# Second half's output projection between the steps of the first half's h, and a later x scaling and earlier rope angles, in a two-block fp32 transformer

## The chip, the cores and the metric

One core of one Trainium2 chip. The metric is the device time of one execution in microseconds (us), the median of several runs.

## What is computed

Two transformer blocks on one sequence of 1024 tokens of width 1024, everything in fp32. The first block has two layers, the second one layer of mixers and a feed-forward part. Cut to what matters here:

```python
# first block: layer 0 is differential attention, layer 1 latent attention; 8 heads each
for i in range(2):
    shift, scale, gate = modulation(c, ada_w[i], ada_b[i])
    h = rmsnorm(x, norm_g[i]) * (1 + scale) + shift
    y = attention_i(h, positions, ...)        # ends in: (o * silu(z)) @ w_out[i]
    x = x + gate * y
x = rmsnorm(x, final_norm_g)
# second block
cos, sin = rope_tables(positions_2)           # cos, sin of positions_2 * inv_freq
h = rmsnorm_2(x, g_mix) * (1 + scale1) + shift1
y = mixers(h @ w_in, cos, sin, ...) @ w_out   # gating, stick-breaking, dilated windows
x = x + (1 + gate1) * y
h = rmsnorm_2(x, g_ffn) * (1 + scale2) + shift2
x = x + (1 + gate2) * feed_forward(h)
return rmsnorm_2(x, g_final)
```

## The kernel before

x is held transposed (features on the 128 partitions, eight tiles of 128 features) and in two halves of 512 tokens. An fp32 product is made of three matmuls on rounded upper parts and their remainders (`mm3`, L192: upper by upper, upper by lower, lower by upper), so one output tile of 128 features by 512 tokens, with eight blocks of the sum, is 24 matmuls 128x512. A weight block comes by a DMA from SyncE (L182), its upper part by a cast on ScalarE (L183), its lower part by a subtraction on GpSimd (L169, through `lo`).

A layer's end is written like this. `out_proj` is a generator with eight steps for a half: weights, 24 matmuls, `scalar_tensor_tensor` on VectorE that adds the gated result to x (the eviction, L781), squares on ScalarE and their sum (`stat_acc`: L372 for the first, L375 and the add L376 for the others), and after some steps a store of x (L788). When a half is done, `stat_sum` casts the sum of squares to an upper part on ScalarE (L383), and two matmuls with ones sum it over the partitions (L386, L387); logarithm and exponential give the root (L393, L394). `make_h` then makes the next layer's input in eight steps: a product on VectorE (L424), for even steps an activation and a subtraction on VectorE (L433, L434), for odd ones two operations on ScalarE and the subtraction on GpSimd (L429, L430, L169). In layer 1 the sum has two forms (with and without the second gain) and three more small operations (L1194, L1195, L1197), and behind make_h eight `scalar_tensor_tensor` scale x for the second block's residual (L1200), followed by stores of it (`move_xt`, L412) and, for the first half, by the rope tables of `positions_2`. The rope tables (L250 to L279) are angles reduced on VectorE (nine operations on 128x1024), then an absolute value, a table load, two sines and a table load on ScalarE.

The code of a layer's end is written half by half: all of the first half's projection, its statistic and h, then all of the second half's. The order in which the engines run is not that: a scheduler puts instructions of the program on each engine by the order of the code and by when it thinks that inputs and buffers are ready, within a priority window, and packs the tiles into SBUF by their lifetimes. Each engine then works strictly in its order, SyncE's queue of DMAs too. Behind the first block, `mixers` begins with two steps of `mixer_a` (its gate, L1215 to L1218, and a normalisation with L1247, L1255 to L1261) before the first queries and keys.

## Time and profile before

| what | us |
|---|---|
| median of three runs | 2959.03 |
| lowest and highest run | 2955.31, 2968.55 |
| the profiled execution itself | 2964.13 |
| span in its trace | 2962.4 |
| TensorE busy in the span | 2646.8 |
| mean granted TensorE clock (1 is full) | 0.951 |

TensorE is busy for 89% of the span. VectorE has 71%, ScalarE 49%, GpSimd 44%. A share is an average over stages with different limits, so the rows further down are taken from single stages: from the ends of the two layers, and from the start.

### The profile page before, as it was taken

The page shows a single profiled execution, that of the slowest core. Times are in us where ns is not written, and L with a number is a line of the kernel's source. Part 1 is how long each engine was busy: PE and PEld are TensorE (multiplying, and loading weights), DVE is VectorE, ACT ScalarE, POOL GpSimd, SP SyncE. Part 2 cuts the span into 40 slices and gives each one's busy share as a digit, 9 for nine tenths or more (in the row PEclk, how much of TensorE's full clock was granted, in tenths as well). Part 3 has the DMA queues.
Part 4 walks back from the last instruction along what each step waited for, and adds up shares of the span by engine and source line. Part 5 has one row for each costly group of instructions (what it writes and reads, how often), then busy time and mean ns, then how long its engine had stood idle before and what let it go on. Part 6 is the DMA issues. An engine that isn't in the chain of part 4 may idle for free. (4 is left out here: it accounts for less than half of the span.)

```text
span 2962.4 us, 34674 instructions
## 1 busy us (share of the span) xinstructions
PE 2646.8 (89%) x12023; PEld 2136.0 (72%) x12023; DVE 2118.1 (71%) x2888; ACT 1437.1 (49%) x2609; POOL 1291.4 (44%) x775
## 2 busy tenths in 40 slices
PE   7889999899889989999987798887887999997897
PEld 4677777777777767787876587776776777775776
DVE  7687677766653377777677665578868888889874
ACT  5455455555543445454554454467544444444432
POOL 3233333333253352122234332244547887778760
PEclk8899999999999999999998899999998999998998
DMA  7534323233351263333333237424441222234564
GB/s 270 142 90 114 92 66 110 75 79 100 106 172 58 66 226 120 114 104 103 109 126 94 74 93 104 101 64 126 130 152 42 80 79 78 82 105 161 189 237 143
DMA packets 316850, 338.91 MB, mean 114 GB/s; under 512 B 37684, under 2 KB 240516, under 8 KB 316676
## 3 DMA queue, kind: packets, MB, share of 16 engines
q1 hardware_dynamic: 316676, 336.70, 38.6%
q8 instruction: 96, 1.57, 0.2%
q14 instruction: 78, 0.64, 0.1%
HBM read 231.17 MB, written 60.89 MB: 99 GB/s over the span
## 5 line engine op out<-in xcount | busy, mean ns | idle before, releaser
L192 PE MATMUL m<-h,wh 128*128 128x512 f32 x4744 | 1398.8, 404 | 62.3 <-ACT wh L183 16.2
L192 PEld LDWEIGHTS m<-h,wh 128*128 128x128 f32 x4744 | 910.4, 194 | 270.9 <-ACT wh L183 18.8
L192 PE MATMUL m<-h,wl 128*128 128x512 f32 x1472 | 589.8, 402 | 8.8 <-POOL wl L169 8.8
L169 POOL TENSOR_TENSOR wl<-wr,wh 128x1024 fp32r<-128x1024 f32 (+1 forms) x146 | 330.5, 2270 | 479.0 <-ACT wh L183 183.7
L761 ACT CAST pt<-m 128x256 fp32r<-128x256 f32 (+1 forms) x632 | 222.3, 370 | 289.9 <-PE m L757 158.3
L192 PEld LDWEIGHTS m<-h,wl 128*128 128x128 f32 x1472 | 286.9, 195 | 73.9 <-POOL wl L169 11.2
L169 DVE TENSOR_TENSOR pt<-m,pt 128x256 fp32r<-128x256 f32 (+2 forms) x652 | 256.3, 416 | 83.1 <-ACT pt L761 70.8
L741 ACT ACTIVATE e<-s,cf 128x1024 f32<-128x1024 f32 x192 | 214.9, 1121 | 155.1 <-DVE cf L738 139.1
L737 DVE TENSOR_REDUCE cf<-s 128x1 f32<-128x1024 f32 x192 | 232.4, 1217 | 75.8 <-PE s L682 40.5
L757 PE MATMUL m<-cr,e 128*128 128x128 f32 x1240 | 195.4, 282 | 32.9 <-DVE cf L738 14.3
L865 POOL TENSOR_SCALAR e<-e,cf 128x1024 f32<-128x1024 f32 x64 | 82.0, 1281 | 307.8 <-DVE cf L742 278.1
L192 PE MATMUL s<-h,wh 128*128 128x512 f32 x720 | 183.3, 400 | 36.4 <-DVE h L169 17.1
L681 PE MATMUL s<-kk,qq 128*128 128x512 f32 (+3 forms) x376 | 152.5, 411 | 52.6 <-ACT e L741 24.9
L757 PEld LDWEIGHTS m<-cr,e 128*128 128x128 f32 x1240 | 152.6, 145 | 61.5 <-issue 22.3
L1533 DVE SCALAR_TENSOR_TENSOR e<-z,cf,e 128x1023 f32<-128x1023 f32 (+1 forms) x88 | 175.8, 2008 | 24.8 <-ACT e L1531 24.6
L192 PE MATMUL m<-pt,v 128*128 128x512 f32 x768 | 188.7, 395 | 1.0 <-DVE pt L169 0.5
L192 PEld LDWEIGHTS s<-h,wh 128*128 128x128 f32 x720 | 136.9, 192 | 72.7 <-DVE h L169 18.6
L183 ACT CAST wh<-wr 128x1024 fp32r<-128x1024 f32 (+2 forms) x134 | 122.1, 915 | 110.6 <-PE m L192 47.2
L192 PEld LDWEIGHTS m<-pt,v 128*128 128x128 f32 x768 | 144.4, 190 | 32.3 <-DVE pt L169 1.6
L1105 POOL TENSOR_SCALAR e<-e,cf 128x1024 f32<-128x1024 f32 x64 | 73.7, 1154 | 186.6 <-DVE cf L742 182.7
L682 PE MATMUL s<-kk,qq 128*128 128x512 f32 (+3 forms) x376 | 144.4, 392 | 1.5 <-DMA qq<-pt 1.5
L169 DVE TENSOR_TENSOR wh<-wl,wh 128x512 fp32r<-128x512 f32 x90 | 121.7, 1370 | 19.4 <-ACT wh L443 19.2
(368 smaller groups left out, 4549.2 us busy)
## 6 DMA issues: line engine op xcount, KB each, us to landing
wr<-in_w_out_dram SPq DMA_DIRECT2D x48, 512.0 KB
tb<-in_w_ada_dram SPq DMA_DIRECT2D x48, 512.0 KB
wr<-in_w_up_dram SPq DMA_DIRECT2D x47, 512.0 KB
wr<-in_w_in_dram SPq DMA_DIRECT2D x45, 512.0 KB
qq<-ab SPq DMA_DIRECT2D x144, 128.0 KB
wr<-in_ada_w_dram SPq DMA_DIRECT2D x32, 512.0 KB
tf<-act SPq DMA_DIRECT2D x30, 512.0 KB
wr<-in_w_down_dram SPq DMA_DIRECT2D x30, 512.0 KB
```

Of the source, the lines that this page charges most:

```text
L169: (eng or self.nc.vector).tensor_sub(lo, src, hi.bitcast(F32))
L183: nc.scalar.copy(hi, raw)
L192: self.nc.tensor.matmul(out, l, r, start=start and n == 0, stop=stop and n == last)
L681: nc.tensor.matmul(ps, q(0, j), kk[:, ks], start=True, stop=False)
L682: nc.tensor.matmul(ps, q(1, j), kk[:, ks], start=False, stop=stop)
L737: nc.vector.reduce_max(nm, ps, axis=AX, negate=True)
L741: nc.scalar.activation(e, ps, AF.Exp, bias=nm, scale=scale, accum_out=sm)
L757: nc.tensor.transpose(ps[:, i], p[:, kt * 128:(kt + 1) * 128], self.ident)
L761: nc.scalar.copy(hi, ps[:, i:i + m])
L865: nc.gpsimd.tensor_scalar(e1, e1, r1, self.neglam, ALU.mult, ALU.mult)
L1105: nc.gpsimd.tensor_scalar(e, e, r, 1.0, ALU.mult, ALU.mult)
L1533: nc.vector.scalar_tensor_tensor(t[:, sh:], u[:, 0:S - sh], col(i), t[:, sh:], ALU.mult, ALU.add)
```

## The change

Four edits. First, `make_h` becomes a generator (`steps_h`); at both layers' ends two of the eight steps of the second half's projection are emitted before the first half's statistic, and the other six alternate with the eight steps of the first half's h. Second, in layer 1 the scaling of x and its stores go to a generator `keep_x` that is emitted in the mixers, alternating with the first queries, keys and values. Third, the rope tables are split into angles and sines; those of `positions_2` are emitted before layer 1's last head's projection (behind `drain(mods)`), with the angles on GpSimd: a cast, multiplications, a subtraction, three pairs of a multiplication into a tile of its own and an addition, and a clamp, eleven operations. Two operations on the way are fused into one, in the first table too. Fourth, two steps of the first queries go between the first two steps of `mixer_a`.

```diff
     def rope_tables(self, nme):
+        self.rope_sin(self.rope_angles(nme, self.nc.vector))
+
+    def rope_angles(self, nme, eng):
...
-        nc.vector.tensor_scalar_mul(k, ang, 1.0 / two_pi)
-        nc.vector.tensor_scalar_add(k, k, magic)
-        nc.vector.tensor_scalar_sub(k, k, magic)
+        eng.tensor_scalar(k, ang, 1.0 / two_pi, magic, ALU.mult, ALU.add)
+        eng.tensor_scalar_sub(k, k, magic)
         for cc in (c1, c2, c3):
-            nc.vector.scalar_tensor_tensor(ang, k, -cc, ang, ALU.mult, ALU.add)
-        nc.vector.tensor_scalar(ang, ang, lim, -lim, ALU.min, ALU.max)
+            if eng is nc.vector:
+                eng.scalar_tensor_tensor(ang, k, -cc, ang, ALU.mult, ALU.add)
+            else:
+                t = self.t("e", [128, S])
+                eng.tensor_scalar_mul(t, k, -cc)
+                eng.tensor_add(ang, ang, t)
+        eng.tensor_scalar(ang, ang, lim, -lim, ALU.min, ALU.max)
+        return ang, k
+
+    def rope_sin(self, angles):
...
     def make_h(self, xt, rr, acol, bcol, scaled=None):
-        nc = self.nc
         out = []
+        drain(self.steps_h(out, xt, rr, acol, bcol, scaled))
+        return out
+
+    def steps_h(self, out, xt, rr, acol, bcol, scaled=None):
...
             out.append((h[:, 0], h[:, 1]))
-        return out
+            yield
...
-        res = []
+        res = [[], []]
         for half in range(2):
             drain(proj[half])
-            res.append(self.make_h(xbox[half][1], self.stat_end(acc[:, half], D), acol, self.mod["shift1"]))
+            if half == 0:
+                drain(some(proj[1], 2))
+            steps = self.steps_h(res[half], xbox[half][1], self.stat_end(acc[:, half], D), acol, self.mod["shift1"])
+            drain(steps if half else alternate(steps, some(proj[1], 6)))
         return res
...
         drain(mods)
+        self.phase = 2
+        self.rope_sin(self.rope_angles("positions_2", nc.gpsimd))
+        self.phase = 1
...
-        hts = []
+        hts = [[], []]
+        self.later = []
         for half in range(2):
             drain(proj[half])
+            if half == 0:
+                drain(some(proj[1], 2))
...
-            hts.append(self.make_h(xt, rf, acol_f, m2["shift_m"]))
-            for c in range(8):
-                nc.vector.scalar_tensor_tensor(xt[c], xt[c], fg[:, c:c + 1], rr, ALU.mult, ALU.mult)
-            self.move_xt(self.xs2, half, tiles, True)
-            if half == 0:
-                self.rope_tables("positions_2")
+            steps = self.steps_h(hts[half], xt, rf, acol_f, m2["shift_m"])
+            drain(steps if half else alternate(steps, some(proj[1], 6)))
+            self.later.append((half, tiles, xt, rr))
         return hts
+
+    def keep_x(self, half, tiles, xt, rr):
+
+        fg = self.col["final_norm_g"]
+        for c in range(8):
+            self.nc.vector.scalar_tensor_tensor(xt[c], xt[c], fg[:, c:c + 1], rr, ALU.mult, ALU.mult)
+            yield
+        self.move_xt(self.xs2, half, tiles, True)
...
         box, vbox = [], []
+        first = qkv(0, box, vbox)
         next(ma)
+        drain(some(first, 2))
         next(ma)
-        drain(alternate(qkv(0, box, vbox), some(ma, 4)))
+        drain(alternate(alternate(first, some(ma, 4)), chain(*(self.keep_x(*x) for x in self.later))))
```

What the scheduler makes of it is seen best at three places. In the rows a line is that of the program they are from; the changed program's lines are 13 to 33 higher from `make_h` on (L424 is L441 there, L434 is L451, L781 is L798, L788 is L805, L376 is L389, L741 is L758; the scaling L1200 is L1233).

SyncE at layer 0's end, before: loads for the next layer (`in_w_in1`), the store of the second half's first tile of x (L788), the last three blocks of the projection's weights (`in_w_out0`).

```order
L182 DMA wr_1223_7696<-in_w_in1_dram 128x8x128
L182 DMA wr_1232_7762<-in_w_in1_dram 128x8x128
L788 DMA xs1_6129<-pt_1135_7087 128x2x512
L182 DMA wr_1165_7272<-in_w_out0_dram 128x8x128
L182 DMA wr_1170_7308<-in_w_out0_dram 128x8x128
L182 DMA wr_1175_7343<-in_w_out0_dram 128x8x128
L788 DMA xs1_6129<-pt_1136_7088 128x2x512
```

The same place now:

```order
L805 DMA xs1_6128<-ab_1047_6560 128x2x512
L182 DMA wr_1153_7211<-in_w_out0_dram 128x8x128
L805 DMA xs1_6128<-pt_1121_7038 128x2x512
L182 DMA wr_1159_7251<-in_w_out0_dram 128x8x128
L182 DMA wr_1166_7292<-in_w_out0_dram 128x8x128
L182 DMA wr_1172_7332<-in_w_out0_dram 128x8x128
L182 DMA wr_1194_7431<-in_w_in1_dram 128x8x128
L182 DMA wr_1197_7438<-in_w_in1_dram 128x8x128
```

The store (L805) is still ahead of the last three weight blocks, but it is that of the two products that are emitted first, and the next layer's loads come behind all of the projection's weights.

VectorE at layer 1's end behind the first half's statistic, before (kk is the first half's x, pt the second's, z the statistic, tf and h4 the products and parts of h):

```order
L1197 TENSOR_TENSOR z_1969_12087<-z_1969_12087 128x512
L424 SCALAR_TENSOR_TENSOR tf_2111_12870<-kk_2031_12379,cf_226,z_1969_12087 128x512 x2
L424 SCALAR_TENSOR_TENSOR tf_2114_12880<-kk_2032_12380,cf_226,z_1969_12087 128x512 x2
L424 SCALAR_TENSOR_TENSOR tf_2117_12890<-kk_2033_12381,cf_226,z_1969_12087 128x512 x2
L424 SCALAR_TENSOR_TENSOR tf_2120_12900<-kk_2034_12382,cf_226,z_1969_12087 128x512 x2
L781 SCALAR_TENSOR_TENSOR pt_2127_12940<-m_2138_12988,cf_226,pt_2127_12940 128x512
L1200 SCALAR_TENSOR_TENSOR kk_2031_12379<-kk_2031_12379,cf_226,z_1969_12087 128x512 x2
L1200 SCALAR_TENSOR_TENSOR kk_2032_12380<-kk_2032_12380,cf_226,z_1969_12087 128x512 x2
L434 SCALAR_TENSOR_TENSOR h4_2112_12872<-tf_2111_12870,cf_226,h4_2112_12872 128x512
L1200 SCALAR_TENSOR_TENSOR kk_2033_12381<-kk_2033_12381,cf_226,z_1969_12087 128x512 x2
L1200 SCALAR_TENSOR_TENSOR kk_2034_12382<-kk_2034_12382,cf_226,z_1969_12087 128x512 x2
L781 SCALAR_TENSOR_TENSOR pt_2128_12941<-m_2144_13026,cf_226,pt_2128_12941 128x512
```

The same place now:

```order
L1223 TENSOR_TENSOR z_1976_12109<-z_1976_12109 128x512
L441 SCALAR_TENSOR_TENSOR tf_2132_12972<-kk_2038_12401,cf_226,z_1976_12109 128x512 x2
L389 TENSOR_TENSOR z_1977_12110<-z_1977_12110,tf_2138_13009 128x512
L798 SCALAR_TENSOR_TENSOR pt_2114_12873<-m_2144_13026,cf_226,pt_2114_12873 128x512
L1233 SCALAR_TENSOR_TENSOR kk_2038_12401<-kk_2038_12401,cf_226,z_1976_12109 128x512
L389 TENSOR_TENSOR z_1977_12110<-z_1977_12110,tf_2139_13012 128x512
L1233 SCALAR_TENSOR_TENSOR kk_2038_12401<-kk_2038_12401,cf_226,z_1976_12109 128x512
L451 SCALAR_TENSOR_TENSOR h4_2133_12974<-tf_2132_12972,cf_226,h4_2133_12974 128x512
L441 SCALAR_TENSOR_TENSOR tf_2147_13058<-kk_2039_12402,cf_226,z_1976_12109 128x512 x2
L389 TENSOR_TENSOR z_1977_12110<-z_1977_12110,tf_2145_13052 128x512
L389 TENSOR_TENSOR z_1977_12110<-z_1977_12110,tf_2146_13055 128x512
```

The eight products of h in one piece (L424) become pairs (L441), with evictions of the second half (L798), its sums (L389) and the scaling of x (L1233) between them.

ScalarE at the start, before the first exponentials of the first attention head, before:

```order
L700 COPY tf_134_854<-m_139_892 128x512
L711 CAST v_132_852<-m_140_918 128x512
L741 ACTIVATE e_151_943,cf_226<-s_150_936,cf_226 128x1024
L741 ACTIVATE e_153_953,cf_226<-s_152_946,cf_226 128x1024
L741 ACTIVATE e_167_1027,cf_226<-s_166_1020,cf_226 128x1024
L183 CAST wh_220_1371<-wr_222_1373 128x1024
```

The same place now:

```order
L717 COPY tf_134_853<-m_139_891 128x512
L288 ACTIVATE e_1969_12081<-e_1970_12083 128x1024
L728 CAST v_132_851<-m_140_917 128x512
L289 ACT_TABLE_LOAD
L289 ACTIVATE tb_1974_12098<-e_1969_12081,cf_226 128x1024
L290 ACTIVATE tb_1975_12099<-e_1970_12083 128x1024
L292 ACT_TABLE_LOAD
L183 CAST wh_220_1370<-wr_222_1372 128x1024
L758 ACTIVATE e_151_942,cf_226<-s_150_935,cf_226 128x1024
L758 ACTIVATE e_153_952,cf_226<-s_152_945,cf_226 128x1024
```

The second rope's absolute value, table loads and sines (L288 to L292), emitted in layer 1, stand here, and with them a weight cast (L183) that stood behind the third exponential.

## Rows read from the trace of the kernel before

**Rows 1.** The page's first table: busy time of each engine, its share of the span and its instructions.
```profile
PE 2646.8 (89%) x12023; PEld 2136.0 (72%) x12023; DVE 2118.1 (71%) x2888; ACT 1437.1 (49%) x2609; POOL 1291.4 (44%) x775
```

**Rows 2.** The timeline of TensorE, 836 to 925 us: the last product of the first half in layer 0. Columns: start and duration in us, engine, line, operation, what it writes and reads, count, and in brackets the idle time before it and what ended that.
```profile
838.87 5.60 PE L192 MATMUL m<-pt,v 128*128 128x512 f32 x24
```

**Rows 3.** Busy time by stretches of 20 us at the end of layer 0. Columns: the stretch, its length, busy time of TensorE (matmuls, number), its weight loads, VectorE, ScalarE, GpSimd, granted clock of TensorE, share of the DMA engines, GB/s; the last row has sums and means.
```profile
860.00:880.00 20.00, 15.48 (x56) 11.25 (x55) 18.40 (x13) 12.10 (x19) 17.28 (x8) 0.83 0.77 231
...
sum 80.00, PE 68.98 PEld 53.27 DVE 40.38 ACT 33.49 POOL 32.36; mean PE 17.25 PEld 13.32 DVE 10.10 ACT 8.37 POOL 8.09
```

**Rows 4.** TensorE's waits, 840 to 925 us: who waited for whom, total in us, times, longest.
```profile
PE m L386 <- ACT tf L383: 4.7, 2, 2.9
PE m L192 <- ACT wh L183: 4.1, 3, 2.8
PE m L192 <- POOL wl L169: 1.8, 1, 1.8
```

**Rows 5.** The timeline of SyncE's queue, 848 to 900 us (start, duration, DMAs issued).
```profile
875.06 0.37 SPq L788 DMA_DIRECT2D xs<-pt  x1
875.52 4.46 SPq L182 DMA_DIRECT2D wr<-in_w_out_dram  x3
```

**Rows 6.** Busy time by stretches of 20 us at the end of layer 1, columns as in rows 3.
```profile
1570.00:1590.00 20.00, 12.20 (x45) 9.64 (x44) 20.00 (x12) 7.51 (x12) 16.82 (x8) 0.76 0.47 126
...
1630.00:1650.00 20.00, 13.28 (x51) 10.53 (x50) 19.81 (x24) 11.86 (x21) 7.76 (x5) 0.83 0.19 73
...
sum 160.00, PE 122.49 PEld 97.39 DVE 110.83 ACT 69.10 POOL 60.02; mean PE 15.31 PEld 12.17 DVE 13.85 ACT 8.64 POOL 7.50
```

**Rows 7.** TensorE's waits, 1540 to 1715 us, columns as in rows 4.
```profile
PE m L192 <- ACT wh L183: 12.1, 2, 7.8
...
PE m L192 <- DVE h L434: 6.7, 1, 6.7
PE s L681 <- ACT kk L1261: 5.7, 1, 5.7
PE m L1247 <- POOL z L1218: 5.6, 1, 5.6
```

**Rows 8.** The timeline of VectorE, 1560 to 1602 us.
```profile
1565.78 16.33 DVE L424 SCALAR_TENSOR_TENSOR tf<-kk,cf,z 128x512 f32<-128x512 f32 x8
1582.03 0.74 DVE L781 SCALAR_TENSOR_TENSOR pt<-m,cf,pt 128x512 f32<-128x512 f32 x1
...
1596.61 0.74 DVE L781 SCALAR_TENSOR_TENSOR pt<-m,cf,pt 128x512 f32<-128x512 f32 x1
...
1599.91 2.68 DVE L376 TENSOR_TENSOR z<-z,tf 128x512 f32<-128x512 f32 x4
```

**Rows 9.** The timeline of ScalarE, 1575 to 1606 us.
```profile
1584.32 1.03 ACT L183 CAST wh<-wr 128x1024 fp32r<-128x1024 f32 x1
```

**Rows 10.** The timeline of VectorE, 1618 to 1645 us: the eight products of the second half's h, when GpSimd had little to do.
```profile
1631.99 6.44 DVE L424 SCALAR_TENSOR_TENSOR tf<-pt,cf,z 128x512 f32<-128x512 f32 x8
```

**Rows 11.** The timeline of TensorE, 1540 to 1720 us: the two statistics, and the first product of the second half's h.
```profile
1551.83 1.41 PE L386 MATMUL m<-tf,cr 128*128 128x512 f32 x2 [4.57 <-ACT tf L383]
...
1618.71 1.35 PE L386 MATMUL m<-tf,cr 128*128 128x512 f32 x2 [3.00 <-ACT tf L383]
...
1644.11 0.80 PE L192 MATMUL m<-h,wh 128*128 128x512 f32 x1 [6.72 <-DVE h L434]
```

**Rows 12.** Groups of VectorE's instructions, 1560 to 1600 us: count, busy us, mean ns of one, idle time before them.
```profile
L424 DVE SCALAR_TENSOR_TENSOR tf<-kk,cf,z 128x512 f32<-128x512 f32 x8 | 16.3, 2108 | 0.0
L1200 DVE SCALAR_TENSOR_TENSOR kk<-kk,cf,z 128x512 f32<-128x512 f32 x8 | 11.3, 1470 | 0.0
```

**Rows 13.** Groups of GpSimd's instructions, 1560 to 1600 us, columns as in rows 12.
```profile
L169 POOL TENSOR_TENSOR wl<-wr,wh 128x1024 fp32r<-128x1024 f32 x8 | 21.4, 2700 | 2.2 <-issue 1.3 <-POOL wr L129 0.9
```

**Rows 14.** Busy time by stretches of 10 us around the second rope angles, columns as in rows 3.
```profile
1490.00:1500.00 10.00, 10.00 (x46) 8.23 (x45) 9.01 (x14) 2.11 (x5) 0.00 (x0) 0.91 0.03 10
```

**Rows 15.** The timeline of GpSimd, 40 to 118 us.
```profile
111.84 1.19 POOL L865 TENSOR_SCALAR e<-e,cf 128x1024 f32<-128x1024 f32 x1 [19.30 <-DVE cf L742]
```

**Rows 16.** The timeline of ScalarE, 1486 to 1510 us: tables and sines of the second rope.
```profile
1501.37 1.28 ACT L276 ACT_TABLE_LOAD   x1
1502.66 1.15 ACT L276 ACTIVATE tb<-e,cf 128x1024 f32<-128x1024 f32 x1
...
1504.78 1.28 ACT L279 ACT_TABLE_LOAD   x1
```

**Rows 17.** The timeline of ScalarE, 92 to 118 us: the first exponentials of the first attention head.
```profile
106.26 1.11 ACT L741 ACTIVATE e<-s,cf 128x1024 f32<-128x1024 f32 x1 [2.88 <-DVE cf L738]
...
113.13 1.11 ACT L741 ACTIVATE e<-s,cf 128x1024 f32<-128x1024 f32 x1 [4.35 <-DVE cf L738]
...
114.83 1.04 ACT L183 CAST wh<-wr 128x1024 fp32r<-128x1024 f32 x1 [0.49 <-DMA wr<-in_w_in_dram]
```

**Rows 18.** The timeline of SyncE's queue, 0 to 110 us.
```profile
107.45 0.44 SPq L182 DMA_DIRECT2D wr<-in_w_in_dram  x1
```

**Rows 19.** The timeline of TensorE, 96 to 118 us.
```profile
114.39 0.80 PE L681 MATMUL s<-kk,qq 128*128 128x512 f32 x1 [6.07 <-ACT e L741]
```

**Rows 20.** TensorE's waits in layer 0's heads, 120 to 840 us, columns as in rows 4.
```profile
PE s L681 <- ACT e L741: 18.8, 13, 3.3
```

**Rows 21.** TensorE's waits in layer 1's heads, 930 to 1540 us.
```profile
PE s L1100 <- DVE h L169: 8.8, 4, 6.2
```

More of the change, by code (lines that the diff above doesn't have):

```diff
@@ L264, in rope_tables @@
         ang = self.t("e", [128, S])
-        nc.vector.tensor_copy(ang, pi)
-        nc.vector.tensor_scalar_mul(ang, ang, inv[:, 0:1])
+        eng.tensor_copy(ang, pi)
+        eng.tensor_scalar_mul(ang, ang, inv[:, 0:1])
         k = pi.bitcast(F32)
-        nc.vector.tensor_scalar_mul(k, ang, 1.0 / two_pi)
-        nc.vector.tensor_scalar_add(k, k, magic)
-        nc.vector.tensor_scalar_sub(k, k, magic)
+        eng.tensor_scalar(k, ang, 1.0 / two_pi, magic, ALU.mult, ALU.add)
+        eng.tensor_scalar_sub(k, k, magic)
         for cc in (c1, c2, c3):
-            nc.vector.scalar_tensor_tensor(ang, k, -cc, ang, ALU.mult, ALU.add)
-        nc.vector.tensor_scalar(ang, ang, lim, -lim, ALU.min, ALU.max)
+            if eng is nc.vector:
[7 more added lines that the diff above has]
+    def rope_sin(self, angles):
+        nc = self.nc
+        ang, k = angles
         cos, sin = self.t("tb", [128, S]), self.t("tb", [128, S])
@@ L416, in make_h @@
     def make_h(self, xt, rr, acol, bcol, scaled=None):
+        out = []
+        drain(self.steps_h(out, xt, rr, acol, bcol, scaled))
+        return out
+    def steps_h(self, out, xt, rr, acol, bcol, scaled=None):
         nc = self.nc
-        out = []
         for c in range(8):
```

## The prediction

> **What bounds the kernel now.** I read the page's first table, then the stretches at the two layers' ends, then TensorE's waits there, then who was late. TensorE is busy 2646.8 us of a span of 2962.4 us, against 71% for VectorE [rows 1], so the span moves only where TensorE stands still, or runs at its lower clock level, now. Its unit is the 128x512 matmul: 24 of them, one product of eight blocks, took 5.60 us [rows 2], 0.23 us each.
>
> Layer 0's end, 840 to 920 us: TensorE is busy 68.98 of 80 us, so 11.0 us idle; and between 860 and 880, at a granted clock of 0.83, its 56 matmuls took 15.48 us where 12.9 would do [rows 3], 2.6 us more. The stops that count are those for weights, 4.1 us for the upper parts and 1.8 us for the lower, and 4.7 us before two statistics, the longer one 2.9 us [rows 4]. The weights were late because SyncE issues in order: loads for the next layer, then a store of the residual that waits for the second half's own results (875.06), and only behind it the last three weight blocks (875.52) [rows 5].
>
> Layer 1's end, 1550 to 1710 us: TensorE is busy 122.49 of 160 us, 37.5 us idle; and in the two stretches shown, at 0.76 and 0.83, its 45 and 51 matmuls took 3.4 us more than 0.23 us each [rows 6]. It waited for casts of weights 12.1 us, for the second half's first h 6.7, for the mixers' key and gate vectors 5.7 and 5.6 [rows 7]. Behind the first of these stands VectorE, busy 20.00 of the 20 us from 1570 [rows 6]: the eight products of h (L424) in one piece took 16.33 us, and the second half's evictions (L781) stood behind them until 1582.03 and then behind scalings of x until 1596.61 [rows 8]. ScalarE takes its work in order too: it made the parts of h as VectorE let it, and only at 1584.32 came the weight cast that TensorE wanted [rows 9].
>
> **The change, part by part.**
>
> *Layer 0's end: 5 us gained.* Two products of the second half (11 us) now stand before the first half's statistic, and all second-half weights before the next layer's loads. The weight stops, 4.1 + 1.8 = 5.9 us [rows 4], go. The first statistic's stop, 4.7 - 2.9 = 1.8 us, does not: the statistic stands behind the 48th of those matmuls, and its cast on ScalarE behind squares of the second half's newest block, so the chain is an eviction, squares, an add and a cast, as at the other statistic, where it cost 2.9: 1.1 us lost. That other one has two L424 and an L434 of the first half's h ahead of its last add, 0.8 us each where VectorE has them to itself [rows 10], in part while it would wait anyway: 1.3 us lost. Of the 2.6 us of low clock I give back 1.5. Together 5.9 - 1.1 - 1.3 + 1.5 = 5.0. Ends: 8 (no new stop) and 1 (the new stops take nearly all).
>
> *Layer 1's end up to the second half's statistic: 12 us gained.* The second half's eight products are 192 matmuls, 44 us; with the first statistic they took from 1547.26 (1551.83 less its stop of 4.57) to 1618.71, 71.5 us [rows 11]. Now two products run at once (to 1558.3), the statistic waits some 4.5 us (the 4.57 us now; its chain is as long), so stands at about 1563, and six products follow: at TensorE's own pace the second statistic would come near 1600 with its stop. But VectorE makes h, and the first L424 came 14.0 us behind the statistic's matmul [rows 8, 11], so 1577 now. From there it has 8 L424, 8 scalings, 4 L434, four evictions and nine adds. Beside GpSimd's work an L424 took 2.04 us and a scaling 1.41 [rows 12]; with the L434 at the scaling's price that is 33 us, and 16 us at the 0.8 us that an L424 takes alone [rows 10]. Evictions at 0.74 and adds at 0.67 [rows 8] make 9. So VectorE ends between 1602 and 1619. GpSimd's weight parts, 21.4 us [rows 13], can in part run in the 14 us before the first L424, so I take 1607, below the middle: 12 us. Ends: 18 and 0.
>
> *From there to 1710 us: 15 us gained.* TensorE's first product of the second half's h came 25.4 us behind the statistic [rows 11]; of what it does in between there are now 12 matmuls more, 2.7 of the 6.7 us stop. The gate and key vectors, 5.6 and 5.7 us [rows 7], were asked for soon after the products that they come from; now 48 and more matmuls of another product stand in between, 11 us, and both are covered. Lost: the second statistic's stop grows by 2.5 us, since 2 L424, 2 scalings and an L434 of the first half's last step stand before its last add. Low clock goes with the stops [rows 6]; I give back 3.5 us. 2.7 + 5.6 + 5.7 - 2.5 + 3.5 = 15. Ends: 20 and 5.
>
> The scaling of x brings nothing by itself: for the second half its place on VectorE stays, for the first half the eight stand between steps of h, as counted. Its stores go out later, and are read again a whole mixer stage later.
>
> *The second rope angles: 3 us lost.* Taking them off VectorE near 1490 us gives nothing, since TensorE is busy 10.00 of 10 us there [rows 14]. But the scheduler puts them at the program's start. GpSimd gets eight instructions of 1.2 us [rows 15] and three of up to 2.7 [rows 13], 17 us, among lower parts of the first h and up to the 19.30 us in which it was idle [rows 15]. ScalarE gets an absolute value, and two table loads and two sines, which took 1501.37 to 1506.06, 4.7 us [rows 16], and behind them a weight cast, all before the first exponential, which ran at 106.26 [rows 17]. That cast ran at 114.83 [rows 17], when its load, issued at 107.45 [rows 18], had landed; the load now goes out eight rows earlier, say at 103, so the cast ends near 111.5 and the first exponential is 5 us later. TensorE's stop of 6.07 us there [rows 19] ended with the third exponential, which had itself waited for VectorE until 113.13 [rows 17], so most of the 5 us is hidden. I take 3. Ends: 0, and 10 (all of it passes and GpSimd's part delays h).
>
> A rule weighs on that block. In the trace the second step of it, a sine, begins 0.01 us behind the end of the table load, and a load takes 1.28 us [rows 16]. The Trainium skill, "ScalarE: Activation LUTs", section "What ACT_TABLE_LOAD costs", adds a drain of about 1.38 us to every switch of tables; by it the block would be 2.8 us longer and this term near 5. No gap in the row shows that drain, so the row stands.
>
> **The sum.** 5 + 12 + 15 - 3 = 29. The profiled run took 2964.1 us (1.7 beside its span); the median of the runs is 2959.0, with 13 us between lowest and highest. 2964.1 - 29 = 2935; from the median it would be 2930; I write 2932.
>
> **The rivals.** A change of 0.5%, 14.8 us, is about what a measurement of this kernel can tell from none.
>
> *VectorE stays the bound at layer 1's end.* If all 20 of those instructions run at the price that they had beside GpSimd, the second statistic comes at 1619 and that term is 0: 2932 + 12 = 2944, and with the stop behind it at its worse end 2950. For it: 2.04 against 0.80 us for an L424 [rows 10, 12], and GpSimd's work does not shrink. Against: what stands in pieces delays one eviction at a time. The Trainium skill, "GPSIMD Engine Reference", section "8. Key points", says that GpSimd shares its SBUF interfaces with VectorE and contends with VectorE instructions that have two SBUF inputs; the trace agrees (an L424 has two, an L781 one, and that took 0.74 us [rows 8]).
>
> *The start costs all its 10 us:* 2932 + 7 = 2939.
>
> *Slower: the second sine and cosine tables lie in SBUF from 100 us to the mixers.* Before, they were made at 1502 us [rows 16]; now 1 MB is held through both layers' heads, and where a prefetch or a probability tile then finds its slot taken, a head waits. TensorE waits little there now: the longest groups are 18.8 us over layer 0's heads and 8.8 us over layer 1's [rows 20, 21]. Sixteen heads that each lost 3.3 us, the longest wait of the first group, would give 53 us: 2932 + 53 = 2985. It decides from 1.8 us a head on, which eats the 29. Against: counted by the tiles' first and last use in the program's order, 48 to 51 of some 52 slots of 4 KB are taken at the fullest places of the heads; two more fit at most of them.
>
> *It does not do what it says:* the order on the engines shows the products moved, so 0.02 only, at 2962.
>
> **How the numbers follow.** Forecast (2918 to 2944) 0.61, VectorE still the bound 0.20, dear start 0.09, slots 0.08, nothing moved 0.02. The range: at the good end 8 + 18 + 20 - 0 = 46 less than 2959 and a little clock, some 2910; at the bad end it takes in the first two rivals and the lower ends of two terms, 2954. Faster by over 0.5% (under 2944): 0.61 x 0.95, half of 0.20 and 0.06 make 0.74; slower 0.08; the rest, 0.18, within.
>
> **What would show it.** Right: no stop for weights between 865 and 885 us; the second half's evictions 5.5 to 7 us apart behind layer 1's first statistic; the second statistic some 60 us behind the end of the first half; no stops for gate and key vectors. Wrong: that statistic still 70 us behind; the first exponential after 112 us with TensorE's work behind it over 3 us later; or waits in the heads above those of [rows 20, 21] by tens of microseconds.

## The result, and the profile after

The changed kernel took 3001.99 us (median; 2996.95 to 3006.59, four runs) against 2959.36 for the kernel before on the same chip: ratio 1.0139, interval 1.0123 to 1.0156, so 41 us slower. The forecast was 2932, the range ended at 2954. The profiled execution has a span of 2999.5 us. TensorE runs the same 12023 matmuls. It is busy for 9.6 us more, at a mean granted clock of 0.941 (0.951 before), and the rest of the 37.1 us are waits [rows 1].

The page's first table, after:

```profile
PE 2656.4 (89%) x12023; PEld 2149.6 (72%) x12023; DVE 2115.2 (71%) x2878; ACT 1437.7 (48%) x2609; POOL 1304.1 (43%) x786
```

Where the time went is seen best by numbering the matmuls in both traces and taking the later start of the same number, in us (positive: later than in the kernel before). The columns are the time in the kernel before. Between 1560 and 1710 us the order differs, so there the two statistics are compared by their own rows. The other rows of the table are runs that are told of below.

| run | 139 | 850 | 925 | 1524 | 1713 | 1778 | 1854 | end |
|---|---|---|---|---|---|---|---|---|
| after | 13.6 | 27.4 | 20.4 | 20.2 | 12.5 | 26.7 | 38.9 | 37.4 |
| e1, rope alone | 14.9 | 26.2 | 25.0 | 28.3 | 29.1 | 30.7 | 34.2 | 31.9 |
| e7, two tiles held | -1.9 | 26.5 | 24.7 | 25.9 | 25.0 | 25.1 | 24.3 | 28.3 |
| e2, mixers' edit alone | -2.1 | -1.4 | 0.4 | 1.3 | -2.7 | 7.7 | 19.7 | 17.6 |
| e14, that with two waits removed | -2.2 | -1.1 | 0.2 | 1.2 | -2.9 | -3.1 | 2.7 | -5.8 |
| e3, ends alone | -1.1 | -0.7 | -4.9 | -5.6 | -10.4 | -8.8 | -5.0 | -7.0 |

So the change loses 13.6 us before the first head is under way and 13.8 in layer 0's heads, gains 7.0 at layer 0's end, loses nothing in layer 1's heads, gains 7.7 at layer 1's end, and loses 24.9 behind it. (Of the lines shown here, L386 is L399 in the changed kernel, L681 is L698, L1427 is L1458; e3 and e8 have numbers of their own.)

**The start.** TensorE's waits, 80 to 140 us, after (who waited for whom, total in us, times, longest):

```profile
PE s L698 <- DMA kk<-ab: 11.5, 3, 4.4
PE m L192 <- POOL h L169: 4.5, 1, 4.5
```

The same two in the kernel before:

```profile
PE s L681 <- DMA kk<-ab: 3.5, 2, 2.6
PE m L192 <- POOL h L169: 0.8, 1, 0.8
```

GpSimd's timeline, 40 to 110 us, after (start, duration, line, operation, idle before it):

```profile
51.34 3.70 POOL L270 TENSOR_SCALAR e<-e,cf 128x1024 f32<-128x1024 f32 x1
55.13 1.19 POOL L272 TENSOR_SCALAR e<-e 128x1024 f32<-128x1024 f32 x1
...
80.19 3.10 POOL L279 TENSOR_SCALAR e<-e 128x1024 f32<-128x1024 f32 x1
83.38 2.38 POOL L169 TENSOR_TENSOR wl<-wr,wh 128x1024 fp32r<-128x1024 f32 x1
85.70 2.35 POOL L280 TENSOR_TENSOR e<-e,e 128x1024 f32<-128x1024 f32 x1
88.00 1.27 POOL L169 TENSOR_TENSOR h<-tf,h 128x512 fp32r<-128x512 f32 x1
...
104.20 1.04 POOL L281 TENSOR_SCALAR e<-e 128x1024 f32<-128x1024 f32 x1
```

An L279 multiplies a tensor by one number and takes 2.8 to 3.1 us. The L272 and the L281 apply two numbers in one pass, read and write as much, and take 1.19 and 1.04. VectorE does not make this difference: it was busy all through the L272, and in e5 below, where the same operations run at another time, three L279 take 2.8 us each, the middle one with VectorE busy for 0.2 us of it:

```profile
1457.91 8.48 POOL L279 TENSOR_SCALAR e<-e 128x1024 f32<-128x1024 f32 x3
```

The row that the working took its price of 1.2 us from (L865, [rows 15]) is of the form with two numbers. The eight operations on one tensor took 19.5 us where 9.6 were counted, and all eleven 26.6 where 17 were. Between them stand the lower parts of weights and of h that others wait for. In the kernel before those rows read:

```profile
68.64 2.84 POOL L169 TENSOR_TENSOR wl<-wr,wh 128x1024 fp32r<-128x1024 f32 x1
79.63 1.27 POOL L169 TENSOR_TENSOR h<-tf,h 128x512 fp32r<-128x512 f32 x1 [8.15 <-ACT h L430]
```

The weight part came 14.7 us later, the next loads into the raw weight tiles went out at 85.78 instead of 72.47, and the last part of h came 8.4 us later. The first exponential, at 106.26 us before [rows 17], now ran at 117.96.

**Layer 0's heads**, TensorE's waits, 120 to 840 us, after; the first group answers to [rows 20], the other two were 6.2 and 6.3 us before. One group has shrunk: 14.3 us for VectorE's row maxima (L738) are 4.1 now.

```profile
PE s L698 <- ACT e L758: 23.4, 12, 5.6
PE m L399 <- ACT tf L396: 11.4, 9, 2.7
PE m L774 <- DVE e L883: 11.3, 6, 3.2
```

**Layer 0's end** (columns as in [rows 3]): the 56 matmuls that stood in the 20 us from 860 to 880 at a clock of 0.83 now run between 890 and 902 us, without a gap and at 1.00. Of TensorE's waits from 855 to 945 us, the only group over 0.5 us is the one for the statistics; those for weights [rows 4] are gone.

```profile
890.00:902.00 12.00, 12.00 (x55) 9.93 (x54) 7.23 (x7) 6.16 (x9) 6.96 (x10) 1.00 0.65 171
```

```profile
PE m L399 <- ACT tf L396: 7.5, 3, 3.4
```

**Layer 1's end.** The two statistics of the changed kernel, which answer to [rows 11], from TensorE's timeline:

```profile
1582.17 1.02 PE L399 MATMUL m<-tf,cr 128*128 128x512 f32 x2 [3.57 <-ACT tf L396]
...
1635.14 0.80 PE L399 MATMUL m<-tf,cr 128*128 128x512 f32 x1 [8.44 <-ACT tf L396]
```

The busy time by stretches, to be set beside [rows 6], and TensorE's waits from 1540 to 1720 us, beside [rows 7]:

```profile
1610.00:1630.00 20.00, 10.65 (x36) 8.31 (x36) 19.42 (x20) 7.70 (x13) 9.33 (x5) 0.83 0.52 151
```

```profile
PE m L399 <- ACT tf L396: 12.3, 3, 8.4
PE s L698 <- DMA kk<-ab: 6.6, 1, 6.6
PE m L192 <- ACT wh L183: 6.3, 1, 6.3
PE m L1278 <- POOL z L1249: 6.1, 1, 6.1
PE m L192 <- DVE h L451: 5.9, 2, 3.2
```

VectorE's groups between the two statistics (count, busy us, mean ns, idle before), beside [rows 12]:

```profile
L389 DVE TENSOR_TENSOR z<-z,tf 128x512 f32<-128x512 f32 x13 | 13.0, 1021 | 0.7 <-ACT tf L388 0.7
L1233 DVE SCALAR_TENSOR_TENSOR kk<-kk,cf,z 128x512 f32<-128x512 f32 x8 | 12.7, 1589 | 0.0
L441 DVE SCALAR_TENSOR_TENSOR tf<-kk,cf,z 128x512 f32<-128x512 f32 x8 | 7.4, 963 | 0.1
L451 DVE SCALAR_TENSOR_TENSOR h<-tf,cf,h 128x512 fp32r<-128x512 f32 x4 | 6.0, 1510 | 0.0
```

The second statistic waits 8.44 us where it waited 3.00, VectorE is full ahead of it, and the stops for the gate and the key are there as before, 6.1 and 6.6 us instead of 5.6 and 5.7.

The means in these groups mix two prices. From 1598.1 to 1613.8 us GpSimd runs six operations without a pause, and VectorE's operations with two inputs in SBUF that run wholly beside them take 2.2 to 2.9 us; with GpSimd idle the same take 0.68 to 0.75. From VectorE's timeline:

```profile
1598.60 2.88 DVE L389 TENSOR_TENSOR z<-z,tf 128x512 f32<-128x512 f32 x1
...
1633.32 0.68 DVE L389 TENSOR_TENSOR z<-z,tf 128x512 f32<-128x512 f32 x1
```

What held up the gate can be read there too. The moved products bring operations of their own, and on VectorE those of the query (the rotation, L627 to L630) stand ahead of the gate's next one (L1246). The square that it needs had ended on ScalarE at 1676.89; VectorE stood idle for the query's matmuls and came to it 5.2 us later:

```profile
1678.63 0.69 DVE L627 TENSOR_TENSOR tf<-m,tb 128x512 f32<-128x512 f32 x1 [7.07 <-PE m L192]
...
1682.10 2.96 DVE L1246 TENSOR_SCALAR tf<-tf 128x512 f32<-128x512 f32 x2
```

The key's square on ScalarE (L1284) ran 12.8 us after its input was copied, behind weight casts and a copy that waited for other products; in the kernel before it was 11.8 us.

**The mixers' start**, TensorE's waits from 1700 to 1890 us, after (the 6.6 us are the key's stop once more), and then before:

```profile
PE m L1458 <- ACT pt L1450: 14.4, 3, 10.6
PE s L698 <- DMA kk<-ab: 6.6, 1, 6.6
PE m L192 <- ACT wh L649: 6.2, 1, 6.2
PE s L698 <- DMA qq<-pt: 5.0, 1, 5.0
```

```profile
PE m L1427 <- ACT pt L1419: 10.3, 4, 6.3
PE m L1427 <- DVE pt L169: 1.7, 2, 0.9
PE s L682 <- DMA qq<-pt: 1.5, 1, 1.5
```

### The profile page after: what moved, and what is told of

Read it like the earlier page. It is cut to its first block, busy times and chain, and to the rows that moved or that the text cites. A ratio compares the mean times of both kernels' runs of the same rounds, so it can differ in the third digit from the quotient of the medians.

```text
span 2999.5 us, 34673 instructions
## 1 busy us (share of the span) xinstructions
PE 2656.4 (89%) x12023; PEld 2149.6 (72%) x12023; DVE 2115.2 (71%) x2878; ACT 1437.7 (48%) x2609; POOL 1304.1 (43%) x786
## 5 line engine op out<-in xcount | busy, mean ns | idle before, releaser
L192 PEld LDWEIGHTS m<-h,wh 128*128 128x128 f32 x4744 | 912.9, 195 | 270.2 <-POOL wh L169 11.8
L758 ACT ACTIVATE e<-s,cf 128x1024 f32<-128x1024 f32 x192 | 214.8, 1121 | 153.9 <-DVE cf L755 118.9
L754 DVE TENSOR_REDUCE cf<-s 128x1 f32<-128x1024 f32 x192 | 231.6, 1216 | 66.1 <-PE s L1123 34.2
L774 PE MATMUL m<-cr,e 128*128 128x128 f32 x1240 | 195.9, 283 | 25.5 <-DVE e L883 11.3
L192 PE MATMUL s<-h,wh 128*128 128x512 f32 x720 | 183.5, 401 | 34.4 <-DVE h L169 17.1
L698 PE MATMUL s<-kk,qq 128*128 128x512 f32 (+3 forms) x376 | 155.8, 419 | 63.7 <-ACT e L758 23.4
L1566 DVE SCALAR_TENSOR_TENSOR e<-z,cf,e 128x1023 f32<-128x1023 f32 (+1 forms) x88 | 175.8, 2008 | 24.8 <-ACT e L1564 24.6
L183 ACT CAST wh<-wr 128x1024 fp32r<-128x1024 f32 (+2 forms) x134 | 122.3, 916 | 106.9 <-DMA wr<-in_w_down_dram 43.7
L699 PE MATMUL s<-kk,qq 128*128 128x512 f32 (+3 forms) x376 | 148.2, 401 | 1.2 <-DMA qq<-pt 1.2
L698 PEld LDWEIGHTS s<-kk,qq 128*128 128x128 f32 x376 | 78.2, 209 | 86.8 <-ACT e L758 30.1
```

What stands on the lines that cost most here:

```text
L183: nc.scalar.copy(hi, raw)
L192: self.nc.tensor.matmul(out, l, r, start=start and n == 0, stop=stop and n == last)
L698: nc.tensor.matmul(ps, q(0, j), kk[:, ks], start=True, stop=False)
L699: nc.tensor.matmul(ps, q(1, j), kk[:, ks], start=False, stop=stop)
L754: nc.vector.reduce_max(nm, ps, axis=AX, negate=True)
L758: nc.scalar.activation(e, ps, AF.Exp, bias=nm, scale=scale, accum_out=sm)
```

## The experiments

Ratios are to the kernel before, run beside each; 1% is 29.6 us.

### Which part loses

e1 keeps only the rope's edit (the second angles' move to GpSimd and to the new place, and the fused operation in both tables), e2 only the mixers' edit (two products between the gated block's first steps, x's scaling where it was), e3 only the two ends, e4 everything but the rope.

```
e1: next_h, layer1 and mixers as before; rope_angles("positions_2", nc.gpsimd) kept
e2: mixers() as changed, without keep_x; all else as before
e3: both drain(some(proj[1], 2)) / alternate(steps, some(proj[1], 6)); all else as before
e4: the change, with   -self.rope_sin(self.rope_angles("positions_2", nc.gpsimd))
                       +if half == 0: self.rope_tables("positions_2")   (old place)
```

> The kernel before with the rope edit alone (angles of positions_2 on GpSimd, in the second phase's pool, emitted before layer 1's last head; one fused operation in both tables); everything else as before. Theory A (the loss ahead of layer 0's end belongs to this edit): 12 us lost up to the first attention head and 15 us in layer 0's heads, nothing behind: 2959 + 27 = 2986, between 2980 and 2993. Rival B (the early tables also cost the 25 us in the mixers, by their slots or by what moved up with them): 3010. Rival C (the heads' 15 us come from the other edits): 2971.

Measured: 2999.63 us, 1.0119 (1.0091 to 1.0147), between the ranges of theories A and B: 26.2 us late at 850 us, as in theory A, and 5.7 more by the end.

> The kernel before with only the mixers' new start: two steps of the first queries between the first two steps of mixer_a. Theory A: this edit alone makes the loss behind layer 1's end, some 25 us: 2984, between 2975 and 2992. Rival B (that loss comes from the early tables or from the order in which h arrives): 2959, within 6. My own price in the prediction for this edit was a gain, from covering the key and gate vectors: 2948.

Measured: 2982.24 us, 1.0060 (1.0044 to 1.0076); all of it behind 1713 us.

> The kernel before with only the second half's projection between the steps of the first half's h, at both layers' ends; scaling of x, rope tables and mixers as before. Theory A: 7 us gained at layer 0's end (as in the changed kernel's trace) and 4 to 14 at layer 1's: 2943, between 2936 and 2949. Rival (h that comes in pieces is what costs the mixers' 25 us): 2965 to 2975.

Measured: 2954.50 us, 0.9967 (0.9952 to 0.9983): a gain, but outside theory A's range and about half of what was expected.

> The changed kernel with the rope tables of positions_2 as before (on VectorE, behind the first half's steps, nothing fused). Theory A: the changed kernel's 3002 less 27: 2975, between 2968 and 2982. Rival B (the tables also cost in the mixers): 2950.

Measured: 2975.74 us, 1.0039 (1.0024 to 1.0054). The parts add up: 1.19 + 0.60 - 0.33 = 1.46% against 1.39% for the whole.

### What the rope's move costs

e5 leaves the angles on GpSimd where the change puts them in the text, but takes their tables from phase 1's pool; e6 puts them on VectorE; e7, e9 and e18 move no rope operation at all and only hold tiles; e10 rearranges the list without holding anything.

```
e5:  -        self.phase = 2
     -        self.phase = 1          (around the second rope in layer1)
e6:  -rope_angles("positions_2", nc.gpsimd)
     +rope_angles("positions_2", nc.vector)
e7:  +held = [t("tb", [128, 1024]) for _ in range(2)]; memset each     (start, phase 2)
     +gpsimd.tensor_add(d[:, 0:1], d[:, 0:1], h[:, 0:1])               (mixers)
e9:  as e7 with one tile
e18: as e7 with two tiles of [128, 8]
e10: -tensor_scalar_mul(k, ang, 1/2pi); -tensor_scalar_add(k, k, magic)
     +tensor_scalar(k, ang, 1/2pi, magic, mult, add)                   (kernel before)
```

> The changed kernel with one edit taken back: the second rope angles are still emitted on GpSimd after layer 1's heads, but in phase 1's pool, not phase 2's, so their instructions stand behind layer 1's heads and no longer in the first 110 us. Theory A (the start and layer 0's heads lose because the twelve GpSimd operations are emitted first, and at their new place there is slack for them): the 26 us of the rope edit go, 2972 to 2980 us, and this trace's projection of layer 0 starts its first exp near 106 us. Rival (GpSimd's slowness beside VectorE costs wherever the angles stand): 2995 to 3005. Second rival (at the place where they stand now they are in the way of layer 1's end): 2980 to 2995, with the loss between 1540 and 1720 us.

Measured: 2982.51 us, 1.0058 (1.0038 to 1.0077), 0.81% less than the change. Matmuls at 139 us are 0.4 us early, not 13.6 late, and 5.3 late at 850. The GpSimd operations now run between 1443 and 1479 us: it was the pool that put them at the start. The number is just above the range of theory A: layer 1's heads, where they now run, lose 6.8 us (0.7 late at 925 us, 7.5 at 1524) in the profiled run, which is itself 7.5 us above the median, so that this part is not shown apart from the noise; the rest is the mixers' share (1.0 early at 1713, 24.8 late at 1854).

> The changed kernel with the second rope angles on VectorE and not on GpSimd; they are still hoisted to the program's start, and the two tables still lie in memory through both layers. Theory A (of the 26 us of the rope edit, 12 to 14 are GpSimd's queue at the start, the other 12 to 15 come out of layer 0's heads, whose order the hoist changes): the start's share goes but for about 7 us of VectorE work, so 2988 to 2996. Rival (GpSimd is all of it, and the heads' loss follows from the late start): 2972 to 2980. Rival (where they stand alone counts, any engine pays): 2998 to 3006.

Measured: 3008.64 us, 1.0137 (1.0100 to 1.0174). Theory A fell, and the time is just above the third theory's range: with VectorE the start loses 5.7 us at 139 us instead of 13.6, but at 850 it is 38.8 late, 15.0 of that at the place of a single stop that e7 has too. GpSimd costs the start some 8 us; taking it away does not make the move cheap.

> The kernel before with two tiles of the tables' kind (128 x 1024, 4 bytes) taken at the start and held to the mixers; there is one GpSimd fill of each, and one column of each is read at the mixers. No rope operation is moved. Theory A (the heads of layer 0 lose 12 to 15 us because the list of instructions is arranged anew around two tiles that are held, whatever fills them): 2970 to 2978 us, the loss between 140 and 850 us. Rival (what the heads lose follows from the late start of the cast weights and GpSimd's queue): within 4 us of the kernel before, 2955 to 2966.

Measured: 2990.96 us, 1.0080 (1.0053 to 1.0106). Nothing is moved, the start loses nothing, and by 850 us the kernel is 26.5 us late. TensorE's waits of e7, 120 to 840 us:

```profile
PE s L681 <- ACT e L741: 25.7, 15, 5.5
PE m L757 <- DVE e L866: 9.2, 5, 3.3
...
PE m L192 <- DVE pt L169: 5.6, 2, 3.0
```

and the last head's, 800 to 880 us, the line on what made its idle time:

```profile
  DVE e L866: 12.5, 1
```

There the products that should fill the head's gaps ran in one piece ahead of them, and then TensorE stood 12.5 us for one tile of probabilities. At that place, 820 to 830 us of the kernel before, e7 falls back by 15.0 of the 28.4 us that it loses in these heads. The change and e1 lose nothing there (27.6 and 26.1 us late on both sides), so that e7's loss is not a measure of what the room costs the change.

> The kernel before with one tile of the tables' kind held from the start to the mixers, and not two as in the run that held two and took 2991 us. Theory A (room decides: each held tile takes slots from the heads' prefetches, and the list is packed worse the fewer there are): a part of the 24 us, 2968 to 2980 us, in layer 0's heads again. Rival (a second tile is the one too many, the first finds a free slot): 2955 to 2966. Rival (any new arrangement of the list costs about as much): 2980 to 2993.

Measured: 2980.67 us, 1.0069 (1.0050 to 1.0087). By the time, one tile costs nearly what two do, just beyond theory A's range, and by the number alone the third theory would do. The place is another: the trace is 5.7 us late at 850 us, where e7 is 26.5 late, 11.7 at 1713 and 15.3 at the end.

> The kernel before with two VectorE steps of the rope angles fused into one, which is also in the change. Nothing is held and nothing moved by hand, but the list of layer 0's heads is arranged anew in some 200 places of VectorE, TensorE and ScalarE. Theory A (the loss of the heads comes from the room that the tables take, and a new arrangement by itself is harmless): 2955 to 2968 us. Rival (the arrangement of before was a lucky one, and any other loses): 2970 to 2985.

Measured: 2969.35 us, 1.0022 (1.0007 to 1.0037), 5.4 us late at 850 us: between the two ranges. A new arrangement by itself can cost some 5 us here. e5 runs layer 0's heads in e10's order, but for two places of TensorE's, and loses the same 5.7 us there: what it loses is the fused operation's, not the moved angles'.

> As the run that held two tiles of 4 KB per partition from the start to the mixers (2991 us, 1.008), with two tiles of 32 bytes per partition: the same two fills and two adds on GpSimd, and the order on the engines is that of the kernel before but for a few rows. Theory A (the room decides): 2957 to 2967 us, within 0.2% of the kernel before. Rival (the fills and the long-lived tile's waits cost, whatever its size): 2980 to 2995.

Measured: 2959.74 us, 0.9987 (0.9977 to 0.9998). The same instructions with small tiles cost nothing, and the matmuls of layer 0's heads run in the order of the kernel before. So it is the room that brings e7's loss, by way of the order: with 4 KB slots per partition missing, the list comes out in another order, with more waits. How dear that order is does not follow the number of slots: 28.4 us in these heads for two tiles, 7.0 for one, and 5.7 in e10 for none. Which transfer or tile misses the slot was not shown.

### Layer 1's end

e8 is e3 without the scaling of x.

```
-for c in range(8):
-    nc.vector.scalar_tensor_tensor(xt[c], xt[c], fg[:, c:c + 1], rr, mult, mult)
```

> The kernel with the two layers' ends alone (second half's output projection between the steps of h), without x's scaling by the final norm at layer 1's end: the unscaled x is stored for the residual, a part of the computation is left out. Sixteen VectorE operations of 128 x 512 with two inputs go, eight of them ahead of the second half's statistic. Theory A (VectorE is the bound of layer 1's end, so that emitting matmuls earlier brought 4 us and not 27): the second statistic comes 5 to 11 us earlier than with the scaling, 2943 to 2950 us. Rival (ScalarE's evictions or the statistic's own chain bind there): within 3 us of the ends alone, 2951 to 2958.

Measured: 2948.57 us, 0.9940 (0.9923 to 0.9956). The time is theory A's, the place is not: from the first to the second statistic it is 50.5 us, and in e3 52.6, the second comes at 1610.39 us where e3 has it at 1608.98, and the gain comes behind it (17.1 us early at 1713, e3 10.4). VectorE's groups between the two statistics, of e3 and then of e8 (count, busy us, mean ns, idle before):

```profile
L1210 DVE SCALAR_TENSOR_TENSOR kk<-kk,cf,z 128x512 f32<-128x512 f32 x8 | 12.7, 1592 | 0.0
L376 DVE TENSOR_TENSOR z<-z,tf 128x512 f32<-128x512 f32 x13 | 10.9, 853 | 0.8 <-ACT tf L375 0.8
L428 DVE SCALAR_TENSOR_TENSOR tf<-kk,cf,z 128x512 f32<-128x512 f32 x8 | 9.5, 1228 | 0.1
```

```profile
L376 DVE TENSOR_TENSOR z<-z,tf 128x512 f32<-128x512 f32 x14 | 15.3, 1129 | 3.0 <-ACT tf L375 3.0
L428 DVE SCALAR_TENSOR_TENSOR tf<-kk,cf,z 128x512 f32<-128x512 f32 x8 | 10.2, 1318 | 0.1
```

12.7 us of scalings go, 12.0 of them ahead of the second statistic, and from statistic to statistic VectorE is busy 39.2 us instead of 43.4 (the rows' windows reach a little past the second one). GpSimd has 25.4 and 25.5 us of work there; where scalings stood beside it, additions and products now do, and an addition takes 1.13 us in the mean instead of 0.85.

### The mixers' start

In e2 ScalarE's waits from 1700 to 1870 us hold two on stores:

```profile
ACT tf L1214 <- DMA od<-tf: 13.2, 1, 13.2
...
ACT cf L1438 <- DMA lse<-cf: 11.5, 1, 11.5
```

The first is new: the gated block's result (L1280) was made at 1700.9 us before and at 1715.3 now, because two products run ahead of the block, and the square of the second block (L1214) needs the tile that this result is stored from. The second was there before, 12.1 us.

```
e11: e2,  nc.sync.dma_start(od[b, ...], y)  ->  nc.gpsimd.dma_start(od[b, ...], y)
e12: e4 with that edit
e13: e2,  y = self.t("tf", ...)  ->  y = self.t("ab", ...)
e14: e13, and "ld": (16, 1) -> (16, 2): two sets of columns for the softmax sums
e15: e4 with both edits of e14
e16: e3 with the second edit of e14
e17: e15, and the sums' stores of dilation 4 and 16 by nc.gpsimd.dma_start
```

> The mixers' edit alone (first projections ahead, as in the run that took 2982 us), with the four stores of the gated block issued by GpSimd's queue and not SyncE's. Every engine's order of work is the same otherwise. Theory A (the 20 us come from that store: in SyncE's order it stands behind the store of the softmax sums and two weight loads, and ScalarE waited 13.15 us for it at 1733): that stop goes, 2964 to 2972 us. Rival (ScalarE's waits are only shifted, TensorE was short of casts anyway): 2978 to 2985.

Measured: 2981.60 us, 1.0071 (1.0046 to 1.0095). Theory A fell: the store was issued at 1710.3 us from the other queue, ScalarE waited 13.1 us for it all the same. The four such stores took 3.7 to 17.2 us to land.

> The changed kernel without the second rope angles' move (the run that took 2975 us), with the four stores of the gated block on GpSimd's queue. Theory A (that store is what turned the 16 us gained up to 1713 us into a loss in the mixers): 2952 to 2962 us, and the sum of the parts that are left, ends and mixers, is then a gain or nothing. Rival (the mixers' loss is in the products' order itself): 2970 to 2978.

Measured: 2972.99 us, 1.0047 (1.0032 to 1.0062), no different from e4.

> The mixers' edit alone (2982 us), with the stored half of the gated block in a tile of kind ab and not tf; the order on the engines is the same but for a few rows. ScalarE's square of the second gated block no longer waits for that store to land (13.2 us at 1733). Theory A (two products ahead make the block, and so its store, 13 us later, and a tf tile comes free so much later): TensorE's stop of 6.0 us for a cast at 1744 goes, 2970 to 2978 us. Rival (the order of the products itself, whatever the tiles): 2979 to 2985.

Measured: 2977.03 us, 1.0042 (1.0025 to 1.0059). TensorE's stop for the cast (L632) falls from 6.0 to 1.4 us, and at 1750 us the kernel is 2.5 us early where e2 was 6.4 late. By 1854 us that is spent: from 1713 us on it loses 21.5 us, and e2 22.4. The intervals of e2 and e13 overlap, so that this edit's share by itself is not shown.

> As the run before it, and the softmax sums of two heads in two sets of columns, not one, so that ScalarE no longer waits for the first set's stores (11.5 us at 1828). Theory A (these two waits are the mixers' loss): the stops of 10.4 us for a probability tile and 6.4 us for the query's heads near 1831 to 1857 go too, 2955 to 2966 us. Rival (the stores' wait was as long before the change, so it isn't the loss): as e13, within 4 us.

Measured: 2964.52 us, 1.0003 (0.9988 to 1.0018): the mixers' loss is gone with both edits; the second alone was not run on e2. Its TensorE waits from 1700 to 1890 us:

```profile
PE s L681 <- DMA qq<-pt: 12.7, 1, 12.7
PE m L1427 <- ACT pt L1419: 2.8, 3, 1.1
```

> The changed kernel without the second rope angles' move (2975 us), with both tile edits of e14. Theory A: what was gained up to 1713 us, 16 us, is kept: 2938 to 2952 us. Rival (the products' order loses in the mixers whatever the tiles): 2966 to 2976.

Measured: 2958.63 us, 0.9972 (0.9959 to 0.9985): better than e4 by 0.67%, but half of the 16.2 us that it is early at 1778 us is given back. The next in line is late, the third head's query, whose transfers stand on SyncE behind eight stores of sums (11.05 us) and a first transfer that took 10.07 us to issue. TensorE's longest wait there, e15, and of e17 the same:

```profile
PE s L685 <- DMA qq<-pt: 14.4, 1, 14.4
```

```profile
PE s L685 <- DMA qq<-pt: 9.1, 1, 9.1
```

> The two layers' ends alone (2954 us) with two sets of columns for the softmax sums. Theory A (in the kernel before, too, ScalarE's 12.1 us wait for those stores near 1815 makes TensorE's stop of 6.3 us): 2944 to 2951 us. Rival (something else is late there as well): within 3 us of 2954.

Measured: 2958.97 us, 0.9973 (0.9957 to 0.9989): no gain over e3. The wait of 12 us for the sums' stores cost nothing where it always stood; taking it from e13 was worth 0.39%, some 12 us. That it counts there because the work ahead of it is late is a reading; no run separates it.

> The run of ends, mixers' edit and both freed tiles (2958.6 us), with the 12 stores of the softmax sums of the second and third dilated pairs of heads issued by GpSimd and not SyncE. SyncE spent 11.05 us on eight of them and then 10.07 us on the next head's first transfer, and TensorE stopped 14.4 us for that head's query at about 1840. Theory A (SyncE's order is what makes the query late): the stop falls to 5 us or less, 2944 to 2953 us. Rival (4-byte elements keep the DMA engines busy whichever queue they come from; the query is as late): 2955 to 2963. Rival (GpSimd pays for issuing them, and what stands behind on it is late): 2964 to 2975.

Measured: 2952.98 us, 0.9967 (0.9955 to 0.9979). The time is at the upper end of theory A's range, the mechanism is not its own: the stop falls to 9.1, not to 5, and the kernel is 17.7 us early at 1854 us where e15 was 7.1, but only 7.2 at the end: most of it is given back by 2000 us. From e15 and from e3 its time can't be told apart. So four versions, e3, e15, e16 and e17, beat the kernel before by 0.3%, and the ends are all that they have in common.

## Why the prediction was wrong, step by step

- **Layer 0's end, 5 us gained: right.** 7.0 in the change, 4.2 in e3; the stops for weights are gone, as forecast, and those for statistics are 7.5 us where the working has 4.7 + 1.1 + 1.3 = 7.1.
- **Layer 1's end to the second statistic, 12 us: wrong, the first rival was right.** 3.8 were gained (20.2 us late ahead of it, 1635.14 - 1618.71 = 16.4 at the statistic). Less the 20.2 us that is 1614.9, where the working had 1602 to 1619 and took 1607. The first product of h came 14.7 us behind the statistic, as taken (14.0), and VectorE then needed some 38 us where 30 were taken. The products of h were cheap (0.96 us, between the two prices of the working); what was mis-sized are the additions, 12 of 1.05 us behind that first product where nine of 0.67 were counted, 6.6 us more, and scalings of 1.59 instead of 1.41. The working had two prices for the products and the additions at the lower one alone. All of them are dear beside GpSimd, so that in e8 additions and products became dearer when the scalings went.
- **From there to 1710 us, 15 us: wrong.** 3.9 were gained. The covers failed: with other products put between, the stops for gate and key stayed as long (6.1 and 6.6). In e3, without the mixers' edit, they are 5.6 and 5.7, so neither form of the order hid them. The working counted TensorE's time between asking and wanting, and not that the moved products' own operations stand in VectorE's order ahead of the gate's. That is read from the trace; no run has another order.
- **The rope, 3 us lost: this step failed worst.** 27 us were lost up to 850 us, and 24 of the 41 go when only the pool is changed (e5). Two things failed. The price: eight GpSimd operations were put at 1.2 us each from a row of another form and took 19.5 us together, and the first exponential came 11.7 us later, not 5; 13.6 us were lost at the start. And the order: the working let the heads run as before, and they lost 13.8 us more. It priced the tables' room as a rival at 0.08 with a reason against it, the count of free slots. e7 and e18 show that room can cost layer 0's heads 28 us, and the change lost nothing in layer 1's (20.4 and 20.2 us late at both ends), so it is not 3.3 us a head. How much of the change's 13.8 us is room stays open: 5.7 us are lost in e10 and e5 with the fused operation and no room taken, and 15.0 of e7's come at a stop that the change does not have.
- **Behind 1710 us: priced at nothing, without a reason, 24.9 us lost.** The sum ended where the moved products end. The block that they were moved ahead of is a chain (product, square, transposes, store, next square) that came 14 us later, and its store's landing, and the sums' stores behind it, then stood in ScalarE's way. Freeing both tiles takes e2's loss away (e14); how it divides between the two is not shown.

That x's scaling brings nothing by itself was not tested: no run moves it alone.

## What to carry to other kernels

When an edit lengthens the life of a tile, price the room first: compare the order of the engines far from the edit, and hold an idle tile of that size to measure it before moving any work. Price an operation from a row of the same form, and VectorE's by what GpSimd does beside it, not by a mean. When work is moved ahead of a chain, follow the chain to the landing of its last store and to whoever needs that tile next; the sum must not end where the moved instructions end. A wait that costs nothing at its old place (the sums' stores) can cost all of its length once what stands behind it is on the path.

## What the runs showed of the hardware

- GpSimd's operations with a tensor and one number (L270, L273, L279; 128x1024) took 2.78 to 3.70 us each in the change and 2.77 to 2.85 in e5, one of those with VectorE busy for 0.2 us of it; with two numbers (L272, L281) 1.04 to 1.36 in both. No run changes the form alone.
- VectorE's operations with two inputs in SBUF (128x512) took 0.68 to 0.75 us with GpSimd idle, and 2.2 to 2.9 where they ran wholly beside its unbroken work (the change, 1598.1 to 1613.8 us; one addition beside a later, single GpSimd operation took 0.68). The evictions, with one input in PSUM, took 0.74 to 0.75 in both cases. Taking 12.0 us of such work away in e8 saved VectorE 4.2.
- A 256 KB store from GpSimd's queue took 3.7 to 17.2 us to land (e11); from SyncE's, ScalarE waited until 1733.6 us for one of two issued between 1716.1 and 1718.1 (e2). Eight stores of sums in 4-byte pieces held SyncE's issue for 18.0 us in the kernel before and 11.05 in e15.
